# First attention stage of a hybrid decoder layer: pool layout, chained second minimum, inverse sums on GpSimd

## The chip, the cores and the metric

The kernel runs on one core of one Trainium2 chip. The metric is device microseconds of one execution, as the median of several runs; lower is better. The core has five instruction streams that run side by side, each in its own fixed order: TensorE (PE in the profile, with its weight loads as PEld), VectorE (DVE), ScalarE (ACT), GpSimd (POOL) and SyncE (SP, which only issues transfers). An instruction starts when the one before it on its engine has gone and the semaphores that it names have come.

## The reference, cut to what matters

One decoder layer over 1024 tokens of width 1024. A token mixer with two head groups is followed by a SwiGLU network. The change lies in group A (8 heads, 2 key groups of 4 heads), whose output is a gated sum of three softmax attentions:

```python
p_c = _masked_softmax(einsum(qg, kc) * scale, mask_c)      # 63 compressed keys per head
imp = einsum(p_c, overlap)                                 # picks 8 blocks of 64 keys per query
p_s = _masked_softmax(einsum(q_b, kg) * scale, mask_s)     # the selected blocks
p_w = _masked_softmax(einsum(q_b, kwb) * scale, mask_w)    # a sliding window of 512 keys
o = gt[:, :, 0] * o_cmp + gt[:, :, 1] * o_s + gt[:, :, 2] * o_w

def _masked_softmax(s, mask):
    s = where(mask, s, NEG_INF)
    e = where(mask, exp(s - max(s)), 0.0)
    return e / maximum(sum(e), 1e-30)
```

Group B (8 heads) is a second attention over 256 picked keys per query, with the same softmax.

## The kernel before, in words

The program is one long function. It runs in stages: conditioning and norm; projections with the top-k search of group B beside them; the first attention stage (group A); the second attention stage (group B, `DsaUnit`); output projection; the feed-forward network. A scheduler orders each engine's instructions from the written program by priorities, so the order of the source is not the order on an engine.

**The first attention stage** has 32 units, `NsaUnit(i, g, br)`: query tile `i` of 128 tokens (0 to 7), key group `g`, branch `br` (2 is the window, 1 the selected blocks). A unit has two halves. `head` (L804) makes four rows of scores, one per head. For each, `softmax_head` (L715) lets PE write scores of up to 512 keys into a PSUM tile `pS` (L721, L723), and DVE reads it once: one pass adds the mask, scales by -0.125, writes `p4` and leaves the row's minimum in `stat` (L729; the pass shows in the trace as a custom instruction and a short reading of its accumulator). With over 512 keys there are two passes, and a DVE instruction on one number per row takes the lesser of both minima (L731). Then ACT takes the exponential with the sum beside it (L732). `inv_sum` (L735) bounds the four sums from below (L736: on DVE for tiles 0 to 3, on POOL from tile 4 on) and inverts them on DVE (L737), and POOL scales the four rows by inverse and gate (L825). `tail` (L829) turns 128 keys at a time on PE (L837), splits them into two halves for accuracy on ACT (L741) and DVE (L742), and multiplies them with the values `VV` (L841, L842). `cmp_tile(i)` (L749) does the compressed branch of a tile for all 8 heads at once, with its own sums of 128x8 (L766 to L771). Heads run two units ahead of tails.

While tiles 0 to 3 run, DVE also writes the last masks of the top-k search (`masks`, L490 to L508).

**Memory.** Pools are stacks on two sides of the on-chip memory. At the end of the projections the right-hand pools `wk` (scratch of the rotation: `rt1`, `rt2`, `tke`), `wstream` (weights `wsp`, raw weights `raw`) and `hT` (the normed input, read by every projection) are closed, and `OT0`, `nsaK` and `att` are opened over their places. An instruction that writes a tile of a new pool waits for the last use of whatever old tile lay there. In the kernel before, tiles of `att` get their places in the order in which the code first asks for them: the first queries `qst` come to lie over `rt1`, `rt2` and `tke`, and the masks `wmask`, `maskc`, `identr`, `trir` over `hT`. At the far end of the stage the pools of the second attention stage lie over those of the first: the raw output weights `rawo1` over `oev`, which POOL reads last of all (L857).

## Time and profile before

| what | value |
|---|---|
| median of 3 runs | 1550.92 us (1549.51 to 1552.92) |
| the profiled execution, its own time | 1550.34 us |
| span of its profile | 1548.4 us |
| PE busy | 93% of the span |
| DVE busy | 76% |
| ACT busy | 57% |
| POOL busy | 45% |
| the chain that ended last | PE 59%, DVE 22%, DMA 6%, ACT 6%, issue 5%, POOL 3% |

Shares over the whole span mix stages with different limits. The first attention stage runs from about 352 to 636 us, the second from there to about 810 us. Times in the trace count from the start of the span.

### The profile page before, as it was taken

Reading aid. Unit: us, or ns where it says so; the run is one execution under the profiler, and the core shown is the slowest. Engines: PE = TensorE matmul, PEld = TensorE weight load, DVE = VectorE, ACT = ScalarE, POOL = GpSimd, SP = SyncE. Lnnn points to the kernel's source line nnn. Section 1 sums busy time; section 2 is a strip of 40 time slices with the busy share of each in tenths; the row PEclk is TensorE's granted clock in tenths of the full one; section 3 lists DMA queues with packets and bytes.
Section 4 is the critical chain, followed back from the end, with each engine's and each line's share of the span. In section 5 each row is a group of like instructions: output and inputs, shape, how many; then the busy total and the mean of one; then the engine's idle time right before and its main releaser. Section 6 shows DMA issues by size and latency. Waiting matters only on the chain.

```text
span 1548.4 us, 23692 instructions
## 1 busy us (share of the span) xinstructions
PE 1439.0 (93%) x7841; PEld 1222.6 (79%) x7841; DVE 1183.7 (76%) x2650; ACT 877.8 (57%) x1848; POOL 703.9 (45%) x978
## 2 busy tenths in 40 slices
PE   3799998996789999899998997999999999999998
PEld 3789898996667877788886785888878888788886
DVE  6888988997999999777865667675775555597757
ACT  3547669876877887677864874222332323354543
POOL 2584353546877666455544524663544353000003
PEclk9999999997999999999999898999999999999999
DMA  9471261200000000210125564542453331784336
GB/s 306 145 246 28 42 175 34 84 11 9 9 12 2 1 13 33 85 35 21 55 69 200 175 222 150 176 147 94 154 165 101 97 109 61 253 276 119 100 111 231
DMA packets 143002, 168.66 MB, mean 109 GB/s; under 512 B 17616, under 2 KB 92720, under 8 KB 142752
## 3 DMA queue, kind: packets, MB, share of 16 engines
q1 hardware_dynamic: 132256, 147.79, 30.3%
q10 hardware_dynamic: 9984, 17.24, 3.3%
q0 software_dynamic: 640, 2.13, 0.5%
q8 instruction: 61, 1.00, 0.3%
q14 instruction: 61, 0.50, 0.1%
HBM read 126.71 MB, written 40.41 MB: 108 GB/s over the span
## 4 chain that ended last, share of the span: by engine, by line
PE 59%; DVE 22%; DMA 6%; ACT 6%; issue 5%; POOL 3%; ACTq 0%; DVEq 0%; SPq 0%; POOLq 0%
PE pT L1158 11%; PE pO L1158 8%; PE pS L1158 6%; PE pT L1400 4%; PE pO L1400 4%; PE pS L1400 3%; DVE tk_j L470 3%; DVE p L729 3%; DVE ptl L742 2%; PE pT L837 2%; PE pO L272 2%; PE pS L721 2%; PE pO L274 2%; PE pO L273 2%; DMA wt<-in_w_ada_dram 2%
## 5 line engine op out<-in xcount | busy, mean ns | idle before, releaser
L742 DVE TENSOR_TENSOR ptl<-pT,ptl 128x512 fp32r<-128x512 f32 x228 | 139.7, 626 | 31.6 <-ACT ptl L741 30.6
L741 ACT CAST ptl<-pT 128x512 fp32r<-128x512 f32 x228 | 117.7, 541 | 40.8 <-PE pO L842 17.7
L1158 PE MATMUL pO<-hbs,wgu 128*128 128x512 f32 x564 | 137.8, 390 | 0.0
L118 ACT CAST wgu<-pair 128x512 fp32r<-128x512 f32 x88 | 53.7, 620 | 137.2 <-PE pT L1158 75.3
L272 PE MATMUL pO<-wsp,hT 128*128 128x256 f32 (+1 forms) x416 | 120.7, 292 | 9.7 <-ACT kvt L607 4.3
L1158 PE MATMUL pT<-hbs,wgu 128*128 128x512 f32 x528 | 127.1, 389 | 1.7 <-DVE u L1305 1.2
L273 PE MATMUL pO<-wsp,hT 128*128 128x256 f32 (+1 forms) x416 | 119.9, 289 | 5.1 <-DVE wsp L121 5.1
L1158 PEld LDWEIGHTS pO<-hbs,wgu 128*128 128x128 f32 x564 | 106.0, 188 | 22.1
L274 PE MATMUL pO<-wsp,hT 128*128 128x256 f32 (+1 forms) x416 | 119.1, 287 | 0.0
L1158 PEld LDWEIGHTS pT<-hbs,wgu 128*128 128x128 f32 x528 | 98.9, 188 | 23.1 <-DVE u L1305 1.6
L825 POOL TENSOR_SCALAR p<-p,stat,gates 128x640 f32<-128x640 f32 (+7 forms) x128 | 106.2, 844 | 23.2 <-DVE stat L737 17.8
L732 ACT ACTIVATE p<-p,stat 128x640 f32<-128x640 f32 (+7 forms) x128 | 94.0, 736 | 26.7 <-DVE stat L731 17.4
L118 ACT CAST wgu<-rawg 128x512 fp32r<-128x512 f32 x66 | 40.9, 622 | 93.8 <-PE pT L1158 48.2
L538 ACT ACTIVATE tk_j<-scores,tk_s 128x384 bf16<-128x384 f32 (+2 forms) x93 | 87.1, 937 | 9.6 <-DVE tk_s L480 3.4
L272 PEld LDWEIGHTS pO<-wsp,hT 128*128 128x128 f32 x416 | 81.0, 196 | 11.8 <-ACT kvt L607 4.9
L118 ACT CAST hl<-adr 128x512 fp32r<-128x512 f32 x77 | 47.4, 621 | 69.8 <-PE pO L1400 31.4
L273 PEld LDWEIGHTS pO<-wsp,hT 128*128 128x128 f32 x416 | 81.3, 196 | 6.7 <-DVE wsp L121 5.8
L121 DVE TENSOR_TENSOR wgu<-pair,wgu 128x512 fp32r<-128x512 f32 x88 | 71.5, 816 | 18.8 <-ACT wgu L118 18.2
L470 DVE TENSOR_SCALAR_CACHE_REDUCE tk_j<-scores,tk_v 128x512 bf16<-128x512 f32 (+2 forms) x96 | 83.9, 874 | 1.1 <-DMA mkd<-tk_j 0.5
L721 PE MATMUL pS<-KK,qst 128*128 128x512 f32 (+3 forms) x192 | 76.1, 402 | 8.3 <-DVE stat L729 8.0
L1411 POOL TENSOR_SCALAR ssd<-ssd 128x1 f32<-128x1 f32 x8 | 2.5, 310 | 178.4 <-ACT pT L1404 177.4
L837 PE MATMUL pT<-ident,p 128*128 128x128 f32 x528 | 81.7, 277 | 1.8 <-POOL p L825 1.2
(497 smaller groups left out, 4566.6 us busy)
## 6 DMA issues: line engine op xcount, KB each, us to landing
rawg<-in_w_gate_up_dram SPq DMA_DIRECT2D x102, 256.0 KB, 3.3
adr<-asd SPq DMA_DIRECT2D x77, 256.0 KB, 2.7
asd<-act SPq DMA_DIRECT2D x66, 256.0 KB, 2.5
raw<-in_w_in_dram SPq DMA_DIRECT2D x36, 256.0 KB, 2.9
xt<-in_x_dram SPq DMA_DIRECT2D x16, 512.0 KB, 6.1
wt<-in_w_ada_dram SPq DMA_DIRECT2D x32, 256.0 KB, 4.4
wt<-in_w_ada_dram SPq DMA_DIRECT2D x16, 512.0 KB, 5.2
we<-in_w_down_dram SPq DMA_DIRECT2D x22, 256.0 KB, 4.8
```

Of the source, the lines that this page charges most:

```text
L118: S.copy(hi, src)
L272: PE.matmul(o, lh, rh, start=first, stop=False)
L273: PE.matmul(o, lh, rl, start=False, stop=False)
L274: PE.matmul(o, ll, rh, start=False, stop=last)
L470: V.tensor_scalar(tkj[0][:, :w], score(i0 + j), thr(j), 0.0, op0=op, op1=OP.add, accum_out=cnt[:, j:j + 1])
L721: PE.matmul(s[:, :c1 - c0], q, kh[:, c0:c1], start=True, stop=False)
L741: S.copy(hl[:n_rows, 0, :width], src[:n_rows, :width])
L742: V.tensor_tensor(hl[:n_rows, 1, :width], src[:n_rows, :width], hl[:n_rows, 0, :width].bitcast(F32), op=OP.subtract)
L825: G.tensor_scalar(self.p4[:, r, :n], self.p4[:, r, :n], stat[:, 2, r:r + 1], gates[:, i, c0 + r:c0 + r + 1], op0=OP.mult, op1=OP.mult)
L837: PE.transpose(pt[:, r * P:(r + 1) * P], self.p4[:, r, k * P:(k + 1) * P], ident)
L1158: PE.matmul(bank, blk[:, a, k, :], hb[:, k, b, :], start=first and k + a + b == 0, stop=k == KH_ - 1 and a == 1, skip_group_check=True)
L1400: PE.matmul(bank[j], A[:, a, j * P:(j + 1) * P], B[:, b, :], start=first and k + a + b == 0, stop=last and k == NP - 1 and a == 1, skip_gr ...
```

## The change

It has three parts.

1. **Places.** `VV` is opened first and all other tiles of the stage go into `att` in the reverse of the order of the table `ATT`, before anything is written. In the built program the first `qst` now lie over the scratch of an earlier projection and the first weight tile of `wstream`, `wmask` over weight tiles, `ce`, `qhl`, `identr` and `trir` over `raw`, and the two large `p4_1` over `hT`; at the other end `rawo0`, `rawo1` and `ohl` of the second stage lie over the second `p4_1`, and no longer over `oev`.
2. **Second minimum.** The second pass over a row starts its minimum from the first pass's result, and writes the row's minimum itself; L731 goes. `softmax_head` also serves the second attention stage.
3. **Inverse sums.** In the first stage POOL takes the bound of all tiles and raises the sums to the power -1 (`OP.pow` with a constant tile), in the units (128x4) and in `cmp_tile` (128x8), where it also multiplies the gate. The second stage keeps its reciprocal on DVE.

```diff
@@ -97,8 +97,10 @@
     addc = cs[:, 320:384].rearrange("p (t e) -> p t e", t=4)
     V.memset(ones, 1.0)
     G.affine_select(ident, ones, pattern=[[1, P]], compare_op=OP.is_equal, fill=0.0, base=0, channel_multiplier=-1)
-    half = cp.tile([P, 4], F32, name="half")
-    V.memset(half, -0.5)
+    half = cp.tile([P, 8], F32, name="half")
+    V.memset(half[:, 0:4], -0.5)
+    V.memset(half[:, 4:8], -1.0)
+    inv = half[:, 4:8]
     tri2 = cp.tile([P, 256], BF, name="tri2")
     tri = tri2[:, 128:]
     G.memset(tri2, 0.0)
@@ -692,11 +694,23 @@
     otp = [R.push("OT0")]
     OT = [otp[0].tile([P, 4, SEQ], F32, name="OT0", tag="o")]
     rK = R.push("nsaK")
-    wmask = rK.tile([P, 640], BF, name="wmask")
-    maskc = rK.tile([P, NT, 64], BF, name="maskc")
-    mask01 = rK.tile([P, 1, 64], BF, name="mask01")
-    trir = rK.tile([P, P], F32R, name="trir")
-    identr = rK.tile([P, P], F32R, name="identr")
+    VV = rK.tile([P, NT, 4, P], F32R, name="VV")
+    at = R.push("att")
+
+    ATT = {"p4_1": ([P, 4, 1024], F32, 2), "trir": ([P, P], F32R, 1), "identr": ([P, P], F32R, 1),
+           "qhl": ([P, 4, 2, 64], F32R, 1), "ce": ([P, 8, 64], F32, 2), "wmask": ([P, 640], BF, 1),
+           "p4_2": ([P, 4, 640], F32, 2), "maskc": ([P, NT, 64], BF, 1), "mask01": ([P, 1, 64], BF, 1),
+           "qst": ([P, 4, P], F32R, 4), "stat": ([P, 4, 4], F32, 4), "st8": ([P, 4, 8], F32, 2),
+           "mr": ([P, 2, 16], F32, 2), "m8": ([P, 2, 8], F32, 2), "imb": ([P, 2, 16], F32, 2),
+           "imh": ([P, 2, 64], F32, 2), "ceh": ([P, 4, 2, 64], F32R, 2), "oev": ([64, 2, 512], F32, 1)}
+
+    def att(name):
+        shape, dt, n = ATT[name]
+        return at.tile(shape, dt, name=name, bufs=n)
+
+    for name in reversed(ATT):
+        att(name)
+    wmask, maskc, mask01, trir, identr = (att(n) for n in ("wmask", "maskc", "mask01", "trir", "identr"))
     G.tensor_copy(identr, ident)
     G.tensor_copy(trir, tri)
     G.memset(maskc, 0.0)
@@ -709,8 +723,6 @@
     G.tensor_copy(wmask[:, 512:], tri)
     G.affine_select(wmask[:, :128], wmask[:, :128], pattern=[[1, P]], compare_op=OP.is_gt, fill=NEG, base=0,
                     channel_multiplier=-1)
-    VV = rK.tile([P, NT, 4, P], F32R, name="VV")
-    at = R.push("att")
     psum_pool("psumB", 512, *ATT_PS)
 
     def softmax_head(p_, q, kh, kl, n, mask, stat, r, diag=False):
@@ -726,15 +738,18 @@
             out_, in_, mk_ = p_[:, c0:c1], s[:, :c1 - c0], mask(c0, c1)
             if diag:
                 out_, in_ = (a.rearrange("p (b e) -> p b e", e=64) for a in (out_, in_))
-            last = V.tensor_tensor_reduce(out_, in_, mk_, -0.125, 3e38, OP.add, OP.min, stat[:, 3 * j, r:r + 1])
-        if n > 512:
-            V.tensor_tensor(stat[:, 0, r:r + 1], stat[:, 0, r:r + 1], stat[:, 3, r:r + 1], op=OP.min)
-        S.activation(p_, p_, AF.Exp, bias=stat[:, 0, r:r + 1], scale=-1.0, accum_out=stat[:, 1, r:r + 1])
+            least = stat[:, 3 * j, r:r + 1]
+            last = V.tensor_tensor_reduce(out_, in_, mk_, -0.125, stat[:, 0, r:r + 1] if j else 3e38, OP.add, OP.min,
+                                          least)
+        S.activation(p_, p_, AF.Exp, bias=least, scale=-1.0, accum_out=stat[:, 1, r:r + 1])
         return last
 
     def inv_sum(stat, eng):
-        eng.tensor_scalar(stat[:, 1, :], stat[:, 1, :], 1e-30, None, op0=OP.max)
-        V.reciprocal(stat[:, 2, :], stat[:, 1, :])
+        G.tensor_scalar(stat[:, 1, :], stat[:, 1, :], 1e-30, None, op0=OP.max)
+        if eng is V:
+            V.reciprocal(stat[:, 2, :], stat[:, 1, :])
+        else:
+            G.tensor_tensor(stat[:, 2, :], stat[:, 1, :], inv, op=OP.pow)
 
     def pT_split(pool, src, n_rows=P, width=512, nb=3):
         hl = pool.tile([P, 2, 512], F32R, name="ptl", bufs=nb)
@@ -765,9 +780,9 @@
             G.tensor_tensor(e, e, mask01.to_broadcast([P, 8, 64]), op=OP.mult)
         V.tensor_reduce(st8[:, 1, :], e, AX.X, OP.add)
         G.tensor_scalar(st8[:, 1, :], st8[:, 1, :], 1e-30, None, op0=OP.max)
-        V.reciprocal(st8[:, 2, :], st8[:, 1, :])
+        G.tensor_tensor(st8[:, 2, :], st8[:, 1, :], inv[:, 0:1].to_broadcast([P, 8]), op=OP.pow)
         if i < 4:
-            V.tensor_tensor(st8[:, 2, :], st8[:, 2, :], gates[:, i, 0:8], op=OP.mult)
+            G.tensor_tensor(st8[:, 2, :], st8[:, 2, :], gates[:, i, 0:8], op=OP.mult)
         G.tensor_tensor(e, e, st8[:, 2, :, None].to_broadcast([P, 8, 64]), op=OP.mult)
         masks = None
         if i >= 4:
@@ -819,7 +834,7 @@
             if self.br == 1:
                 self.eh = at.tile([P, 4, 2, 64], F32R, name="ceh", bufs=2)
                 split(self.eh[:, :, 0, :], self.eh[:, :, 1, :], CM[i][1][:, 4 * g:4 * g + 4, :], S, G)
-            inv_sum(stat, V if i < 4 else G)
+            inv_sum(stat, G)
             c0 = self.br * 8 + 4 * g
             for r in range(4):
                 G.tensor_scalar(self.p4[:, r, :n], self.p4[:, r, :n], stat[:, 2, r:r + 1],
@@ -1024,7 +1039,7 @@
                 mk_ = tri2[:, 128 - P * i:] if i < 2 else score(i, mk)
                 mask = lambda a, b: mk_[:, a:b]
                 softmax_head(self.p4[:, j, :n], qs[tg][:, j, :], KH[:, 0, :], KH[:, 1, :], n, mask, stat, j)
-            inv_sum(stat, G)
+            inv_sum(stat, V)
             for j in range(4):
                 n = (4 * tg + j + 1) * P
                 G.tensor_scalar(self.p4[:, j, :n], self.p4[:, j, :n], stat[:, 2, j:j + 1], 1.0, op0=OP.mult, op1=OP.mult)
```

On POOL, at the start of the stage, the order before (`nqt` is the query tile, L294 to L297 its rotation; `tke` and `mkd` belong to the top-k masks):

```order
L702 MEMSET maskc 128x512
L705 MEMSET mask_4639 128x64
L708 MEMSET wmask 128x512
L709 COPY wmask<-tri_77 128x128
L294 TENSOR_TENSOR rt_4621<-nqt,cs 128x64
L295 TENSOR_TENSOR rt_4622<-nqt,cs 128x4x8
L296 TENSOR_TENSOR rt_4622<-nqt,cs 128x4x8
L703 AFFINE_SELECT maskc<-maskc 128x512
L706 AFFINE_SELECT mask_4639<-mask_4639 128x64
L710 AFFINE_SELECT wmask<-wmask 128x128
L297 TENSOR_TENSOR nqt<-rt_4621,rt_4622 128x4x16
```

and of the change:

```order
L510 DMA mkd<-tke 128x896
L296 TENSOR_TENSOR rt_4622<-nqt,cs 128x64
L297 TENSOR_TENSOR rt_4623<-nqt,cs 128x4x8
L298 TENSOR_TENSOR rt_4623<-nqt,cs 128x4x8
L299 TENSOR_TENSOR nqt<-rt_4622,rt_4623 128x4x16
L714 CAST identr<-ident 128x128
L715 CAST trir<-tri_78 128x128
L716 MEMSET maskc 128x512
L719 MEMSET mask_4662 128x64
L722 MEMSET wmask 128x512
L723 COPY wmask<-tri_78 128x128
L717 AFFINE_SELECT maskc<-maskc 128x512
```

The last rotation now stands ahead of the making of the masks, whose last step is the selection on `wmask` (L724, two rows on); the work is the same.

On ACT at the same place, with the semaphores that each waits for, before:

```order
L305 COPY nqt<-pS 128x256 [waits PE_49]
L402 CAST qst<-pT 64x2x128 [waits PE_49,DMASW0_49,Activation_49,Pool_49]
L403 CAST qst<-pT 64x2x128
L402 CAST qst<-pT 64x2x128 [waits PE_49]
L403 CAST qst<-pT 64x2x128
L118 CAST VV<-kvt 128x8x2x64 x2
```

and of the change:

```order
L307 COPY nqt<-pS 128x256 [waits PE_49]
L404 CAST qst<-pT 64x2x128 [waits DMAHW3_49,DMAHW7_49,PE_49,Pool_49]
L405 CAST qst<-pT 64x2x128
L404 CAST qst<-pT 64x2x128 [waits PE_49]
L405 CAST qst<-pT 64x2x128
L120 CAST VV<-kvt 128x8x2x64 x2
```

The order stays; the first copy into `qst` waits for other transfers (DMAHW3 and DMAHW7 carried results and weights of the projections) and no longer for the one that reads `tke` (DMASW0).

On POOL in the units of tile 0 and 1, before:

```order
L761 TENSOR_TENSOR ce_4696<-ce_4696,st8_4697 128x512
L825 TENSOR_SCALAR p4_2_4719<-p4_2_4719,stat_4720,gates_99 128x128 x4
L765 TENSOR_TENSOR ce_4696<-ce_4696,mask01_4639 128x512
L825 TENSOR_SCALAR p4_1_4747<-p4_1_4747,stat_4748,gates_99 128x128 x4
L121 TENSOR_TENSOR qhl_4828<-nqt_4026,qhl_4828 128x4x64
L508 DMA mkd_92<-tk_j0_487 128x384
L767 TENSOR_SCALAR st8_4697<-st8_4697 128x8
```

and of the change:

```order
L748 TENSOR_SCALAR stat_4739<-stat_4739 128x4
L752 TENSOR_TENSOR stat_4739<-stat_4739,half_75 128x4
L840 TENSOR_SCALAR p4_2_4738<-p4_2_4738,stat_4739,gates_100 128x128 x4
L776 TENSOR_TENSOR ce_4715<-ce_4715,st8_4716 128x512
L748 TENSOR_SCALAR stat_4767<-stat_4767 128x4
L123 TENSOR_TENSOR qhl_4847<-nqt_4027,qhl_4847 128x4x64
L752 TENSOR_TENSOR stat_4767<-stat_4767,half_75 128x4
L780 TENSOR_TENSOR ce_4715<-ce_4715,mask01_4662 128x512
L510 DMA mkd_93<-tk_j0_488 128x384
L840 TENSOR_SCALAR p4_1_4766<-p4_1_4766,stat_4767,gates_100 128x128 x4
L748 TENSOR_SCALAR stat_4798<-stat_4798 128x4
L782 TENSOR_SCALAR st8_4716<-st8_4716 128x8
```

Each set of four scalings now has a bound (L748) and a power (L752) ahead of it in POOL's own queue.

## Rows read from the trace of the kernel before

**Rows 1.** The page: busy time, share of the span and instructions, all engines.

```profile
PE 1439.0 (93%) x7841; PEld 1222.6 (79%) x7841; DVE 1183.7 (76%) x2650; ACT 877.8 (57%) x1848; POOL 703.9 (45%) x978
```

**Rows 2.** Stretches: length, then busy time (count) of PE, PEld, DVE, ACT, POOL; clock; DMA.

```profile
363.20:465.00 101.80, 84.20 (x453) 66.46 (x452) 96.37 (x280) 79.12 (x214) 80.58 (x111) 0.89 0.03 9
465.00:625.00 160.00, 153.60 (x944) 125.34 (x943) 150.90 (x484) 124.40 (x253) 106.36 (x144) 1.00 0.05 16
...
652.00:810.00 158.00, 154.44 (x895) 129.89 (x894) 125.45 (x372) 119.90 (x276) 81.16 (x124) 1.00 0.14 46
```

**Rows 3.** Waits from 355 to 465 us: who for whom; total us, times, longest.

```profile
POOL p L825 <- DVE stat L737: 6.8, 4, 4.2
...
PE pS L721 <- DVE stat L729: 5.3, 8, 1.3
```

**Rows 4.** Waits from 465 to 625 us.

```profile
ACT p L732 <- DVE stat L731: 15.5, 18, 2.7
```

**Rows 5.** Timeline of POOL at the start: start, us, instruction, idle before and releaser.

```profile
355.44 0.30 POOL L700 CAST identr<-ident 128x128 fp32r<-128x128 f32 x1
...
358.70 0.28 POOL L710 TENSOR_SCALAR_AFFINE_SELECT wmask<-wmask 128x128 bf16<-128x128 bf16 x1
358.97 0.31 POOL L297 TENSOR_TENSOR nqt<-rt,rt 128x64 f32<-128x64 f32 x1
```

**Rows 6.** Timeline of PE, ACT and DVE at the same place.

```profile
354.72 0.41 PE L399 MATMUL pT<-ident,nqt 128*128 128x128 f32 x2 [1.63 <-ACT nqt L305]
360.62 0.64 PE L755 MATMUL pT<-KKc,qst 128*128 128x64 f32 x2 [5.49 <-DVE qst L404]
...
359.31 0.37 ACT L402 CAST qst<-pT 64x256 fp32r<-64x256 f32 x1 [4.74 <-POOL nqt L297]
...
363.21 0.29 DVE L729 CUSTOM_DVE_ANT_0 p<-pS,wmask 128x128 f32<-128x128 f32 x1
```

**Rows 7.** DVE's groups from 363 to 625 us: count, busy us, mean ns, idle before.

```profile
L731 DVE TENSOR_TENSOR stat<-stat 128x1 f32<-128x1 f32 x64 | 20.9, 331 | 0.2
...
L736 DVE TENSOR_SCALAR stat<-stat 128x4 f32<-128x4 f32 x16 | 7.0, 440 | 0.0
...
L737 DVE RECIPROCAL stat<-stat 128x4 f32<-128x4 f32 x32 | 5.3, 166 | 0.7 <-POOL stat L736 0.5
```

**Rows 8.** Timeline of DVE at a row with two passes.

```profile
462.09 0.16 DVE L731 TENSOR_TENSOR stat<-stat 128x1 f32<-128x1 f32 x1
462.17 0.28 DVE L729 CUSTOM_DVE_ANT_0 p<-pS,wmask 128x128 f32<-128x128 f32 x1
```

**Rows 9.** Line 127, powers on POOL: ns least, median and most, first and last start.

```profile
L127 POOL TENSOR_TENSOR rxr<-rxv,half x8: 549/722/1355, 10.1 to 46.9; 128x1 f32<-128x1 f32 x8
...
L127 POOL TENSOR_TENSOR rcr<-rcv,half x2: 1115/1561/2007, 74.0 to 87.6; 128x4 f32<-128x4 f32 x2
```

**Rows 10.** Line 736, the bound of the sums, the same columns.

```profile
L736 DVE TENSOR_SCALAR stat<-stat x16: 134/242/1561, 368.4 to 456.4; 128x4 f32<-128x4 f32 x16
L736 POOL TENSOR_SCALAR stat<-stat x16: 219/220/225, 465.8 to 618.9; 128x4 f32<-128x4 f32 x16
```

**Rows 11.** Timeline of POOL at the cheaper power.

```profile
73.97 1.11 POOL L127 TENSOR_TENSOR rcr<-rcv,half 128x4 f32<-128x4 f32 x1
74.98 0.46 POOL L297 TENSOR_TENSOR g<-rt,rt 128x128 f32<-128x128 f32 x1
```

**Rows 12.** POOL's groups from 363 to 465 us: the scaling in its 128x256 form.

```profile
L825 POOL TENSOR_SCALAR p<-p,stat,gates 128x256 f32<-128x256 f32 x16 | 11.6, 736 | 0.0
```

**Rows 13.** Line 825, the scaling, all forms: ns least, median and most.

```profile
L825 POOL TENSOR_SCALAR p<-p,stat,gates x128: 442/878/2425, 370.1 to 623.0; 128x640 f32<-128x640 f32 x40, 128x128 f32<-128x128 f32 x16, 128x256 f32<-128x256 f32 x16, 128x384 f32<-128x384 f32 x16
```

**Rows 14.** The chain that ended last, between the two attention stages.

```profile
639.79 2.56 DMA rawo<-in_w_out_dram
```

**Rows 15.** Timeline of PE at the same place.

```profile
644.24 1.01 PE L1000 MATMUL pT<-ident,dqp 128*128 128x128 f32 x4 [2.43 <-DVE krT L939]
```

## The prediction

> **What bounds the kernel now.** I read the page first: over the whole span DVE is busy 76% and POOL 45% [rows 1]. These are averages over unlike stages, so the second view is the table of stretches, cut where the work changes [rows 2]. It gives the first attention stage in two parts. Stretch A (363 to 465 us, tiles 0 to 3) has DVE busy 96.4 of 101.8 us, POOL 80.6 and PE 84.2: DVE sets the pace, and POOL is the next in line with only 21.2 us free. Stretch B (465 to 625 us, tiles 4 to 7) has PE at 153.6 of 160, DVE at 150.9 and POOL at 106.4: two engines are nearly full, POOL has room. The second stage (652 to 810 us) has PE at 154.4 of 158. The third view is the waits. In A, POOL stands 6.8 us for DVE's reciprocal (L737) and PE 5.3 us for DVE to read a score tile [rows 3]; in B, ACT stands 15.5 us for the lesser of two minima (L731) [rows 4]. The fourth is the timeline where the projections end and the stage starts: PE transposes the first queries at 354.7 us and multiplies them only at 360.6, since ACT may write them no sooner than 359.3, when POOL has ended the last rotation; the first reduction of scores runs at 363.2 [rows 5, 6].
>
> **The change, part by part.** The sum goes against the profiled execution, 1550.34 us, which is 0.6 us (0.04%) below the median, so no correction is made.
>
> *The start.* POOL makes the masks from 355.4 us and ends the last rotation at 358.97 + 0.31 = 359.3, without a pause [rows 5]. The same work in the new order ends at 359.3 too, now with `wmask`. The queries no longer lie over the rotation's scratch, so ACT can write them from about 355.1, when the transposes are through (354.72 + 0.41 [rows 6]), and copies, halves and scores run beside POOL. What the first reduction then waits for last is `wmask`, at 359.3 and not at 363.2: 3.9 us gained. The ends are 0 (another old tile holds the queries as long) and 3.9 (the mask cannot come sooner). I take 3.9, since all that stood in the gap is named by the rows. Late next is that mask.
>
> *Stretch A.* DVE loses 16 bounds, 7.0 us, and 16 of the 32 reciprocals, 5.3 / 2 = 2.7 us [rows 7]; four wide reciprocals and four gate products of one small size are under a microsecond more and left out. That is 9.7 us of DVE. No row has two passes in these tiles. POOL gains 16 bounds at 0.22 us [rows 10], 3.5 us; 16 powers of 128x4; four wide powers of 128x8; four gate products at a price like the bound's, 0.9 us. Powers stand in the trace at L127 alone: 128x1 takes 0.55 us at the least, 128x4 1.115 and 2.007 [rows 9]. These two are the ends. I take the cheaper, as the dearer lies in a place where DVE streams from memory at the same time, and by starts: the next instruction begins 74.98 - 73.97 = 1.01 us later [rows 11]. Sixteen make 16.2 us. For 128x8 I work out (1.115 - 0.549) / 3 = 0.19 us a column, 1.115 + 4 x 0.19 - 0.1 = 1.8 us, four of them 7.1. Together POOL gets 3.5 + 16.2 + 7.1 + 0.9 = 27.7 us and needs 80.6 + 27.7 = 108.3 us where the stretch has 101.8. DVE comes down to 86.7. So POOL takes DVE's place as the bound, and the stretch grows by 6.5 us. Behind a power on POOL stand the four scalings of its unit, then PE's transposes of the tail. Ends: -9.7 us (POOL fits, DVE's relief is all felt) and, with every power as the dearer row, 3.5 + 32.1 + 4 x 3.2 + 0.9 = 49.3 us on POOL, +28 us.
>
> *Stretch B.* DVE loses 64 lesser minima, 20.9 us, and 2.7 us of reciprocals [rows 7]. The chained pass adds a read of the first pass's result on the same engine. Nothing shows that operation. Its nearest row is L731, which waits for the same result: from its start to the next pass 0.08 us [rows 8], 0.33 us on average [rows 7]. These are the ends; I take 0.08, since the long ones are lengthened by something other than that result, and 64 x 0.08 = 5.1 us go back. DVE comes to 150.9 - 20.9 + 5.1 - 2.7 = 132.4 of 160 us. POOL comes to 106.4 + 16 x 1.01 + 4 x 1.8 = 129.8. PE keeps its 153.6 [rows 2], and with DVE out of its way I let the stretch shrink to that: 6.4 us gained. Ends: 0, and 18.5 us (DVE's whole relief, if PE's busy time holds as much hidden waiting).
>
> *The end of the stage.* The load of `rawo1` goes out at 639.8 us, right behind POOL's last sum of the heads [rows 14], because it lies over what that sum reads; ACT's queue holds the copy of that weight ahead of one that PE waits 2.4 us for [rows 15]. In the new places the load waits for neither. The load before it in the queue still has to land, so I take 0.5 us, between 0 and 2.4.
>
> *The second stage.* Another 32 lesser minima go. PE is busy 154.4 of 158 us, so at most 3.6 us can come of it; the cover is PE's filler work, the first half of the output projection. I take 1.5, with ends 0 and 3.6. Its reciprocals stay on DVE and cost what they did.
>
> *Sum.* -3.9 + 6.5 - 6.4 - 0.5 - 1.5 = -5.8 us, 1544.5 us.
>
> **The rivals.**
>
> *POOL becomes a wall (slower).* Mechanism: in tiles 0 to 3 POOL and DVE get in each other's way, so a power costs more than alone. For it: the same scaling of 128x256 takes 0.74 us on average [rows 12], and one scaling took 2.4 us where the least is 0.44 [rows 13]; a bound of four numbers on DVE takes from 0.13 to 1.56 us [rows 10]; one of the two powers is at 2.0. Against it: DVE's 16 bounds go, and they were part of this. Price: with the median of the two powers, 1.56 us, POOL gets 3.5 + 25.0 + 4 x 2.5 + 0.9 = 39.4 us in A and the stretch grows by 18.2; B starts late and gives 4; -3.9 + 18.2 - 4 - 0.5 - 1.5 = +8.3, 1558.6 us. It decides from where A costs 5.8 us more than I took: over 16 powers and four of 1.8 times the size, 0.25 us each, so from 1.26 us a power. The Trainium skill's page Perfetto Trace Analysis, section Optimizing Scalar/DVE Operations, says that GpSimd and DVE share a port to on-chip memory, so that moving work from one to the other might not help; by that rule this rival is the forecast, and the trace agrees in that both engines show the long rows just named.
>
> *POOL is not full (much faster).* Its 80.6 us hold waiting for DVE [rows 12, 13], and with DVE less busy this goes. Then A gains 9.7, B some 12, the second stage 2.5: -3.9 - 9.7 - 12 - 0.5 - 2.5 = -28.6, 1521.7 us. Against it: the work that lengthens POOL's rows, the masks of the top-k, stays.
>
> *The second minimum does not do what it says (no change).* If the chained pass waits for the first as long as L731 took, B and the second stage give nothing: -3.9 + 6.5 = +2.6, 1553 us. For it: in the order both passes of a row can be neighbours. Against it: at L731 the wait itself is 0.08 us.
>
> **How the numbers follow.** The forecast has 0.48, the wall 0.22, no change 0.17, much faster 0.13. About 0.2% (3.1 us) is what a measurement of this kernel can tell from no change. The forecast's own case runs from about 1538 to 1549, and a twelfth of it lies within 3.1 us of the old time. So faster is 0.44 + 0.13 = 0.57, the same 0.04 + 0.17 = 0.21, slower 0.22. The range from 1530 to 1558 leaves out most of the fastest case and the upper half of the wall.
>
> **What would show it.** Right: the first reduction near 359.5 us; in the stretch of tiles 0 to 3 POOL busier than DVE, powers near 1.1 us, and PE's transposes waiting for POOL's scaling; in tiles 4 to 7 ACT's wait for L731 gone and DVE at least 15 us less busy, with PE full. Wrong: powers of 1.3 us or more in the stage, a second pass that takes 0.3 us longer than a first of its size, the first queries still written at 359 us, or DVE still the fullest engine in tiles 0 to 3.

## The result and the profile after

The changed kernel takes 1559.83 us (median of 5 runs, 1558.28 to 1564.86) where the kernel before took 1549.51 beside it: ratio 1.0067 [1.0045, 1.0089]. The forecast was 1544.5 us.

| | before | after |
|---|---|---|
| span of the profile | 1548.4 us | 1558.1 us |
| first reduction of scores | 363.2 us | 357.3 us |
| from there to the end of tile 3's scaling (A) | 101.8 us | 115.5 us |
| from there to tile 7's last product (B) | 171.4 us | 173.1 us |
| last product of the stage to the second stage's first product of probabilities and values (L1044 before, L1059 after) | 28.0 us | 27.8 us |
| first to last such product of the second stage | 169.5 us | 170.4 us |

B ends here at the start of the last product, at 636.4 us before; the 465 to 625 us of [rows 2] lie inside it. The second stage's last product starts at 833.9 us before, behind the 810 of [rows 2].

The page of the changed kernel, busy time of all engines, to be held against [rows 1]:

```profile
PE 1440.7 (92%) x7841; PEld 1226.3 (79%) x7841; DVE 1163.5 (75%) x2495; ACT 879.9 (56%) x1848; POOL 756.9 (49%) x1038
```

Over the span DVE lost 20 us and POOL gained 53. The stretches tell more. A, B and two slices of A in the changed kernel (columns as in [rows 2]):

```profile
357.30:472.80 115.50, 85.54 (x434) 68.55 (x435) 87.32 (x233) 78.03 (x213) 110.52 (x154) 0.81 0.02 8
472.80:645.90 173.10, 166.44 (x1018) 137.05 (x1017) 150.98 (x420) 133.18 (x267) 131.43 (x167) 0.99 0.05 15
380.00:390.00 10.00, 2.88 (x10) 1.91 (x9) 8.10 (x20) 5.05 (x16) 9.52 (x15) 0.54 0.04 15
440.00:450.00 10.00, 4.38 (x15) 2.50 (x15) 3.48 (x10) 3.66 (x10) 10.00 (x14) 0.79 0.01 2
```

In A POOL is busy 110.5 of 115.5 us, DVE 87.3, PE 85.5. From 440 to 450 us POOL works without a break while every other engine is under half. POOL's own waits in A, all of them (who for whom; total us, times, longest):

```profile
POOL stat L748 <- ACT p L744: 0.6, 1, 0.6
```

Before, POOL stood 6.8 us for the reciprocals alone [rows 3]. Now it waits for hardly anybody: 110.5 us of work, 0.6 of waiting and 4.4 in gaps between its 154 instructions are the 115.5. None of these gaps is over 0.11 us. There are 56, and 31 of them stand beside one of the 16 bounds (L748) and make 2.6 us. Elsewhere, as between the four scalings of a unit, an instruction follows the one before it without a gap. In the kernel before there are 19 such gaps in A, 1.4 us. Who waits for it, in the waits from 357 to 475 us:

```profile
PEld pT L861 <- POOL ceh L123: 13.1, 3, 7.7
PE pT L861 <- POOL ceh L123: 12.0, 2, 7.4
ACT ce L777 <- POOL ce L776: 8.2, 3, 6.2
DVE ptl L864 <- PE pT L861: 6.6, 1, 6.6
```

`ceh` (L123) holds the halves of the compressed branch, which the first tails turn on PE (L861). POOL's timeline ahead of the first of them (start, us, instruction):

```profile
374.79 1.64 POOL L783 TENSOR_TENSOR st<-st,half 128x8 f32<-128x8 f32 x1
376.40 1.00 POOL L752 TENSOR_TENSOR stat<-stat,half 128x4 f32<-128x4 f32 x1
377.40 3.12 POOL L840 TENSOR_SCALAR p<-p,stat,gates 128x128 f32<-128x128 f32 x4
380.50 0.64 POOL L785 TENSOR_TENSOR st<-st,gates 128x8 f32<-128x8 f32 x1
...
384.76 1.13 POOL L786 TENSOR_TENSOR ce<-ce,st 128x512 f32<-128x512 f32 x1
...
387.62 1.04 POOL L752 TENSOR_TENSOR stat<-stat,half 128x4 f32<-128x4 f32 x1
388.74 0.64 POOL L782 TENSOR_SCALAR st<-st 128x8 f32<-128x8 f32 x1
389.46 2.85 POOL L123 TENSOR_TENSOR ceh<-ce,ceh 128x256 fp32r<-128x256 f32 x2
```

And PE's at the same place, where the bracket gives the idle time before and its releaser:

```profile
383.45 0.41 PE L735 MATMUL pS<-KK,qst 128*128 128x256 f32 x1
391.24 1.11 PE L861 MATMUL pT<-ident,ceh 128*128 128x128 f32 x4 [7.37 <-POOL ceh L123]
```

The compressed branch's inverse is there at 376.4 us, its gate only behind a power and four scalings at 380.5, its product at 384.8, its halves behind another power at 389.5; and PE does nothing for 7.37 us. The first product with the compressed values (L865, the "first tail" of the expectations) runs at 395 us, where it ran at 388 before (L850), although the stage had started 5.9 us sooner.

Prices of the added instructions, columns as in [rows 9]: the power of a unit, the wide power, the bound. Three groups of the changed kernel:

```profile
L752 POOL TENSOR_TENSOR stat<-stat,half x32: 996/1036/1821, 361.2 to 629.6; 128x4 f32<-128x4 f32 x32
...
L783 POOL TENSOR_TENSOR st<-st,half x8: 1633/1664/1665, 374.8 to 590.4; 128x8 f32<-128x8 f32 x8
...
L748 POOL TENSOR_SCALAR stat<-stat x32: 208/228/547, 360.6 to 629.3; 128x4 f32<-128x4 f32 x32
```

So the power has the price that was taken (1.01 us), and the wide one is a little cheaper than the 1.8 worked out. Two of the sixteen powers in A are longer, 1.42 and 1.82 us.

### The profile page after: what moved, and what is told of

Read it like the earlier page. It is cut to its first block, busy times and chain, and to the rows that moved or that the text cites. A ratio compares the mean times of both kernels' runs of the same rounds, so it can differ in the third digit from the quotient of the medians.

```text
span 1558.1 us, 23702 instructions
## 1 busy us (share of the span) xinstructions
PE 1440.7 (92%) x7841; PEld 1226.3 (79%) x7841; DVE 1163.5 (75%) x2495; ACT 879.9 (56%) x1848; POOL 756.9 (49%) x1038
## 5 line engine op out<-in xcount | busy, mean ns | idle before, releaser
L840 POOL TENSOR_SCALAR p<-p,stat,gates 128x640 f32<-128x640 f32 (+7 forms) x128 | 103.7, 823 | 1.4
L123 DVE TENSOR_TENSOR wgu<-pair,wgu 128x512 fp32r<-128x512 f32 x88 | 72.4, 827 | 18.8 <-ACT wgu L120 18.1
```

What stands on the lines that cost most here:

```text
L123: elo.tensor_tensor(lo, src, hi.bitcast(F32), op=OP.subtract)
L840: G.tensor_scalar(self.p4[:, r, :n], self.p4[:, r, :n], stat[:, 2, r:r + 1], gates[:, i, c0 + r:c0 + r + 1], op0=OP.mult, op1=OP.mult)
```

## The experiments

All times are medians, and each ratio is to the kernel before in runs on the same chip (its medians there 1550.8 to 1551.6 us, and 1549.5 beside the change). "Change" is the whole change, "its order" the order in which the change's engines run.

| kernel | us | ratio | A | POOL busy in A | B |
|---|---|---|---|---|---|
| the change | 1559.8 | 1.0067 [1.0045, 1.0089] | 115.5 | 110.5 | 173.1 |
| places alone | 1549.0 | 0.9986 [0.9974, 0.9999] | 104.2 | 79.4 | 174.1 |
| chained minimum alone | 1546.1 | 0.9979 [0.9965, 0.9992] | 104.3 | 80.6 | 167.1 |
| powers alone | 1572.2 | 1.0148 [1.0124, 1.0171] | 116.8 | 107.5 | 175.5 |
| places and chain | 1543.0 | 0.9955 [0.9934, 0.9975] | 104.1 | 80.4 | 168.7 |
| + power in the units | 1552.5 | 1.0000 [0.9990, 1.0011] | 110.5 | 103.4 | 170.9 |
| + power in the compressed branch | 1549.3 | 0.9986 [0.9973, 0.9998] | 106.5 | 88.9 | 170.7 |
| change, multiplications | 1540.5 | 0.9926 [0.9912, 0.9941] | 97.5 | 90.8 | 169.1 |
| + power from tile 4 on | 1546.4 | 0.9969 [0.9954, 0.9984] | 103.5 | 80.1 | 168.6 |
| its order, all cheap | 1546.5 | 0.9970 [0.9957, 0.9984] | 102.7 | 92.6 | 171.1 |
| other order, all powers | 1572.9 | 1.0134 [1.0115, 1.0153] | 116.5 | 110.1 | 181.7 |
| + spare powers | 1554.8 | 1.0019 [1.0004, 1.0034] | 111.9 | 93.7 | 170.7 |
| places and chain, no bound | 1549.2 | 0.9990 [0.9979, 1.0001] | 103.7 | 82.3 | 173.6 |
| its order, early ones cheap | 1549.7 | 0.9994 [0.9978, 1.0011] | 102.8 | 92.3 | 176.6 |
| its order, early units cheap | 1550.8 | 0.9998 [0.9984, 1.0013] | 104.0 | 99.1 | 174.4 |
| its order, early wide cheap | 1554.9 | 1.0026 [1.0010, 1.0042] | 111.0 | 105.1 | 171.9 |

A and B are of the one profiled execution, "+" means on top of places and chain. That execution can lie some us off the median: 1550.8 us against 1554.9 with the early wide powers cheap, 1542.8 against 1546.4 with powers from tile 4 on.

### The three parts apart

Each of the first three runs is the kernel before with one numbered part of the diff: the table `ATT` (places), the starting value of the second pass (chain), or the powers with their constant tile (powers). The fourth has the first two.

```diff
-    def inv_sum(stat, eng):
-        G.tensor_scalar(stat[:, 1, :], stat[:, 1, :], 1e-30, None, op0=OP.max)
-        if eng is V:
-            V.reciprocal(stat[:, 2, :], stat[:, 1, :])
-        else:
-            G.tensor_tensor(stat[:, 2, :], stat[:, 1, :], inv, op=OP.pow)
+    def inv_sum(stat, eng):
+        eng.tensor_scalar(stat[:, 1, :], stat[:, 1, :], 1e-30, None, op0=OP.max)
+        V.reciprocal(stat[:, 2, :], stat[:, 1, :])
```

(The fourth against the change; the compressed branch's inverse and gate go back to DVE in the same way.)

> The kernel before with the new places alone (part 1 of the change). Theory, POOL is the wall: the places cost nothing and bring the earlier first reduction (357.3 us in the changed kernel, 363.2 before), so 4 to 6 us under the kernel before, about 1544 to 1546 us. Rival, the places are at fault: some tile of the stage now waits longer for an old one, and the loss is already here, at or above 1555 us.

> The kernel before with the chained second minimum alone (part 2). Theory as forecast: VectorE loses some 16 us in tiles 4 to 7 and that is felt, 6 to 8 us under the kernel before. Rival, those tiles are paced by TensorE with its waits for ScalarE's copies: within 2 us of the kernel before although VectorE is busy 15 us less there.

> The kernel before with the inverse sums on GpSimd alone (part 3). Theory, POOL is the wall: this part alone loses, 10 to 16 us over the kernel before, with GpSimd over 92% busy in tiles 0 to 3. Rival, the power is only a loss in the new places, or the scheduler's order did it: within 4 us of the kernel before.

> The changed kernel with the inverse sums back on VectorE (parts 1 and 2, without 3). Theory, POOL is the wall: everything lost comes back and the start stays, 4 to 12 us under the kernel before, 1538 to 1546 us. Rival, places or chain are at fault: still above the kernel before.

Measured: 1549.0, 1546.1, 1572.2 and 1543.0 us. The powers alone lose 1.5%, the other two together win 0.45%, and that pair beats both kernels. Only the pair came out where it was expected: the places gave 1.8 us and not 4 to 6, the chain 4.7 and not 6 to 8, and the powers lost 21 us and not 10 to 16. The places bring the first reduction to 357.6 us, but the last product of tile 2 with the compressed values starts at 448.8 us where it started at 450.4, so most of the start is given back. The chain shortens B: its stretches in the run with the chain alone are

```profile
364.40:468.70 104.30, 88.07 (x452) 70.89 (x452) 95.54 (x278) 79.32 (x214) 80.64 (x111) 0.84 0.03 9
468.70:635.80 167.10, 161.59 (x1011) 134.73 (x1010) 151.12 (x436) 131.13 (x266) 108.89 (x147) 1.00 0.05 15
```

The kernel before has over its own B

```profile
465.00:636.40 171.40, 164.91 (x1011) 134.24 (x1009) 159.53 (x496) 131.92 (x266) 108.72 (x147) 1.00 0.05 15
```

B is 4.3 us shorter, and with the places as well it is 168.7 where the places alone have 174.1. DVE is busy 8.4 us less. PE idles 5.5 us where it idled 6.5, and the other 3.3 us come out of PE's busy time.

### Which of the powers, with a new order each time

"+ power in the units" and "+ power in the compressed branch" put one half of part 3 on top of places and chain. "+ power from tile 4 on" keeps DVE's bound and reciprocal in tiles 0 to 3 and in the compressed branch; of its edit against places and chain, the call (`inv_sum` takes the power where its third argument is true):

```diff
-            inv_sum(stat, V if i < 4 else G)
+            inv_sum(stat, V if i < 4 else G, i >= 4)
```

> The whole change with the compressed branch's inverse and gate put back on VectorE, so GpSimd gets in tiles 0 to 3 only the 16 bounds and the 16 powers of 128x4. Theory 'demand': the loss follows the microseconds that GpSimd must work between the first reduction and the end of tile 3's scaling. Here that is 80.4 (as in the places-and-chain run) + 16 x (1.07 + 0.23) = 101 of some 104 us, so the stretch gives way by half to two thirds of what the whole change does: about 109 us, and a time near 1550 (1546 to 1555). Rival 'queue of the first tails': the loss comes from the compressed branch's own power, which stands in GpSimd's in-order queue ahead of the products for the first tails; without it the first tail is back near 385 us and the time is within 2 us of 1543.

> The whole change with the inverses of the units as before (bound and reciprocal on VectorE in tiles 0 to 3, bound on GpSimd and reciprocal on VectorE from tile 4 on); only the compressed branch's inverse (8 powers of 128x8) and gate are on GpSimd. Theory 'demand': GpSimd has 80.4 + 4 x (1.66 + 0.25) = 88 us of work in a stretch of 104, it is not full, and the time stays at 1543 to 1546. Rival 'queue of the first tails': the power sits ahead of the products that the first tails need; the first tail is 5 us or more later (390 or later instead of 385), and the time is 1549 or more.

> The whole change without any power in tiles 0 to 3 and in the compressed branch: bound and reciprocal on VectorE there, and the power of 128x4 on GpSimd in the 16 units of tiles 4 to 7 alone. Theory 'the loss is made in tiles 0 to 3': GpSimd has 109 + 16 x 1.07 = 127 us of work in tiles 4 to 7's 169, far from full, and the time is that of the places-and-chain run, 1541 to 1546. Rival 'a power costs where it stands too': each power lengthens the chain from a group's sums to its scaling by about 0.9 us against the reciprocal, and tiles 4 to 7 grow by 4 us or more over 168.8; the time is 1547 to 1555.

Measured: 1552.5, 1549.3 and 1546.4 us. The units' powers cost what 'demand' said. With them only in late tiles B stays at 168.6 us in the profiled execution, the fastest of the run; the median, 1546.4, lies between the 1541 to 1546 of the theory and the 1547 to 1555 of its rival and settles neither. The compressed branch alone goes against 'demand': POOL has 88.9 of 106.5 us to do, the first tail runs at 392 us (385 in places and chain), and the time is the rival's. But that difference is 6 us, the scheduler lays a new order for each of the three, and what that alone is worth isn't known yet.

### Price and order apart

The multiplication run replaces `OP.pow` by `OP.mult` at both places (L752, L783) and does not compute the inverse. The first of the two:

```diff
-            G.tensor_tensor(stat[:, 2, :], stat[:, 1, :], inv, op=OP.pow)
+            G.tensor_tensor(stat[:, 2, :], stat[:, 1, :], inv, op=OP.mult)
```

> The whole change with a multiplication in the place of each of the two powers: the same instructions in the same queues in the same order, the inverse is not computed. Theory 'price of the power': with 0.2 to 0.3 us instead of 1.07 and 1.66 GpSimd's work before the end of tile 3's scaling falls from 110 to about 93 us of 104 to 106; the time comes within 3 us of the places-and-chain run, 1542 to 1547. Rival 'order': it is that the sums are waited for by GpSimd's in-order queue instead of by VectorE's; then the price does not matter and the time stays above 1553.

It takes 1540.5 us, less than the 1542 to 1547 of 'price', a ratio of 0.9926 where the change has 1.0067. But what was written ahead of it was wrong in one thing, the order did not stay: the scheduler laid another one, and in the traces near a thousand of PE's 7,841 instructions stand elsewhere. The next two runs keep the orders. The scheduler works on the one operation; when every engine's order is set, the 40 instructions are exchanged for the same ones with the other (`names` holds the 40; the lines that count them are left out):

```diff
+    for f in nc.m.functions:
+        for b in f.blocks:
+            L = list(b.instructions)
+            for k, i in enumerate(L):
+                if i.name in names:
+                    L[k] = type(i)(op=OP.mult, name=i.name, engine=i.engine, debug=i.debug, ins=i.ins, outs=i.outs,
+                                   descendants=i.descendants, sync_info=i.sync_info)
+                    ...
+            b.instructions = L
```

> The multiplication run before this (1540.5 us) also let the scheduler lay every engine's order anew, so price and order changed together. Here each engine's order is word for word that of the whole change, and only the 40 inverses (32 of 128x4, 8 of 128x8) are multiplications when they run; the inverse is not computed. Theory 'price': the order is as good as the other, and the time comes within 4 us of 1540.5, that is 1538 to 1545, with the stretch from the first reduction to the end of tile 3's scaling near 98 us. Rival 'order': the scheduler laid out a worse order around a GpSimd that it believes busy; then the time stays at 1552 to 1560. Between them (1546 to 1551) both have a share.

> The other half of the pair: each engine's order is word for word that of the multiplication run, but the 40 inverses are powers when they run, so it computes what the whole change computes. Theory 'price': 16 x 0.8 + 4 x 1.4 = 18 us more on GpSimd in tiles 0 to 3 than in the multiplication run, most of it on the path: 1552 to 1560. Rival 'order': 1541 to 1546, as in the multiplication run.

The order of the change with cheap inverses takes 1546.5 us (0.9970), with powers 1559.8 (1.0067). The other order takes 1540.5 (0.9926) and 1572.9 (1.0134). In either order the price alone is worth more than the whole loss: 1.0% in the one, 2.1% in the other. 'Price' holds: the second run is even above its 1552 to 1560, and the first, at 1546.5, lies in the zone where both have a share. The change's order is the better one with powers and the worse one without, as if the scheduler had already given way to them. The inverse of a unit in the run of the change's order, cheap:

```profile
L752 POOL TENSOR_TENSOR stat<-stat,half x32: 192/203/998, 362.7 to 616.3; 128x4 f32<-128x4 f32 x32
```

Its stretches A and B:

```profile
358.80:461.50 102.70, 84.46 (x431) 66.69 (x431) 88.16 (x232) 76.06 (x208) 92.58 (x153) 0.83 0.03 9
461.50:632.60 171.10, 165.47 (x1030) 137.20 (x1029) 149.77 (x420) 134.62 (x272) 112.60 (x167) 1.00 0.05 15
```

A is 12.8 us shorter than in the change, with POOL's work 17.9 us less; B only 2.0 us shorter, with 18.8 less. So most of the price is paid in tiles 0 to 3, and the slack of B covers most of it there. PE's wait for the halves of the compressed branch, 12.0 us in the change, is, in the same order with cheap inverses,

```profile
PE pT L861 <- POOL ceh L123: 3.7, 2, 2.7
```

The other order with powers, A and B:

```profile
361.40:477.90 116.50, 86.09 (x420) 71.56 (x420) 87.19 (x230) 75.31 (x207) 110.08 (x150) 0.75 0.02 8
477.90:659.60 181.70, 170.26 (x1040) 139.64 (x1039) 151.03 (x422) 134.16 (x272) 134.09 (x171) 0.98 0.05 14
```

Against the multiplications in that order (97.5 and 169.1 us) A grows by 19.0 us for 19.3 us of POOL's work, and B by 12.6 us for 19.6: what slack B has depends on the order.

The last three keep the change's order and make some of the powers cheap: those of tiles 0 to 3 with five wide ones, the units' among them, the wide ones among them.

> Every engine's order is that of the whole change (1559.8 us). The 16 powers of the units of tiles 0 to 3 and the 5 wide ones of the compressed branch that run beside them are multiplications (their inverses are not computed); the 16 powers of the units of tiles 4 to 7 and three wide ones stay. Theory 'tiles 0 to 3': the loss is made where GpSimd was busy 110.5 of 115.5 us; with these cheap the time is within 3 us of the run with all 40 cheap (1546.5), 1545 to 1550. Rival 'everywhere': the late powers take their share of 13.3 us, some 6 us, and the time is 1551 to 1555.

> As the run before this one, with only the 16 powers of the units of tiles 0 to 3 made cheap. Theory 'a microsecond is a microsecond': GpSimd loses 16 x 0.8 = 13 us of work, the wide ones 5 x 1.4 = 7; the gain over the whole change splits two to one, and the time is 1549 to 1553. Rival 'the wide ones alone count' (they stand ahead of the halves that the first tails wait for): 1556 or more.

> As the two before, with only the 5 wide powers of the compressed branch in tiles 0 to 4 made cheap. Theory 'a microsecond is a microsecond': 7 us less work on GpSimd, a third of the gain, 1554 to 1557. Rival 'the wide ones alone count': 1546 to 1550.

Measured: 1549.7, 1550.8 and 1554.9 us, all inside 'tiles 0 to 3' and 'a microsecond is a microsecond'. 'The wide ones alone count' is out, and the 6 us of the compressed branch alone, in an order of its own, are no sign of it. The early ones carry 0.73 of the 0.97% that all 40 are worth (1.0067 less 0.9994, less 0.9970). The late ones carry the other 0.24%, near what these runs can tell; with them alone B is 176.6 us, 5.5 longer than with all cheap, so B does not cover them for nothing. The early units alone give 9.0 us and the wide ones 5.0, and both together 10.2, less than their sum. Stretch A with the early units cheap, and then with the early wide ones cheap:

```profile
358.80:462.80 104.00, 83.94 (x431) 66.81 (x431) 87.87 (x232) 76.83 (x210) 99.06 (x153) 0.84 0.03 9
```

```profile
357.00:468.00 111.00, 86.82 (x436) 69.09 (x437) 86.98 (x233) 77.88 (x212) 105.12 (x155) 0.80 0.02 8
```

In one order, then, POOL's work of 92.6, 99.1, 105.1 and 110.5 us gives an A of 102.7, 104.0, 111.0 and 115.5. From 99 on the length is the work and 5 to 6 us; below, something else holds some 103, which is why the two parts together give less than their sum. What holds it was not looked for.

### Occupied or in the chain of a unit

The spare powers write a column that nobody reads in tiles 0 to 3; bound and reciprocal stay on DVE.

```diff
         V.reciprocal(stat[:, 2, :], stat[:, 1, :])
+        if eng is V:
+            G.tensor_tensor(stat[:, 3, :], stat[:, 1, :], inv, op=OP.pow)
```

> Places and chain (1543.0 us), with bound and reciprocal on VectorE as before; in tiles 0 to 3 GpSimd takes beside them 16 powers of 128x4 whose results nobody reads. GpSimd's work there goes from 80.4 to about 98 us, as in the run with the units' powers, but no scaling waits for a power. Theory 'GpSimd's hours': what counts is that the engine is occupied, and the time is 1548 to 1554, as with the units' powers (1552.5). Rival 'the chain of one unit': what counts is that bound, power and scaling follow one another on one engine; with the power on nobody's path the time stays at 1542 to 1546.

It takes 1554.8 us, a little over the 1548 to 1554 of 'GpSimd's hours' and 11.8 above places and chain: a power costs as much here when nothing waits for its result. It is not POOL's hours alone, though, since A is 111.9 us with 93.7 of work. POOL's waits in that stretch hold one that the change hasn't:

```profile
POOL stat L751 <- DVE stat L748: 2.3, 4, 1.3
```

The spare power waits for a sum, and all that is queued behind it waits too. That is 2.3 of the 18.2 us in which POOL has no work in this A. DVE is busy 96.3 us where places and chain have 93.0, and the order is new as well, so which of these made A 7.8 us longer stays open.

### A version for use

> A version for use: places and chain, without the bound from below of the units' sums. A row's least scaled score is taken off before the exponential, so one term is exp(0) and the sum is at least 1: the bound of 1e-30 never acts. It takes 16 x 0.32 us off VectorE in tiles 0 to 3 and 16 x 0.22 us off GpSimd in tiles 4 to 7 and the bounds of the second stage. If VectorE's work in tiles 0 to 3 (93 of 104 us in the places-and-chain run) decides there, 1538 to 1541; if the order of waits does, 1541 to 1545 and no difference that these runs can tell.

The run leaves out the bound in `inv_sum`. It takes 1549.2 us, 6 us more than places and chain, though it only takes instructions away: no expectation said that. A is as long (103.7 and 104.1 us), B 4.9 longer. The orders differ throughout, so this is laid to the scheduler's order, but that wasn't tried by itself. It says how far a difference of one edit can be trusted here where the order is laid anew: some 6 us. By that measure the places, the chain, the compressed branch's powers and the late powers, each by a run of its own, are not shown to be worth what their runs differ by; the pairs in one order are. The best version seen is places and chain, 1543.0 us, ratio 0.9955 [0.9934, 0.9975].

## Why the prediction was wrong, step by step

**The start** was small and came in the right direction, 363.2 to 357.3 us, 5.9 gained where 3.9 were taken, but not for the reason given:

```profile
357.32 0.29 DVE L742 CUSTOM_DVE_ANT_0 p<-pS,wmask 128x128 f32<-128x128 f32 x1 [0.18 <-POOL wmask L723]
```

The first reduction needs of `wmask` only the copy of `tri` (L723), through at 357.3. The selection, which the prediction waited for, ends at 359.3 as forecast, but makes a part that tile 0 does not read. Nor is the start set by the places alone: with the same places it is 359.3 in places and chain and 362.7 in the multiplication run, which is the fastest all the same.

**Stretch A is the first of two steps that failed**, in the sentence "So POOL takes DVE's place as the bound, and the stretch grows by 6.5 us". POOL did take it, and the prices were right: 29.9 us of work came to it where 27.7 were counted, a power at 1.04 us. But the stretch grew by 13.7 us, from 101.8 to 115.5. The sum took POOL's 108.3 us of work for the length of the stretch. The work came to 110.5, and a queue that hardly waits still has 4.4 us of gaps, with 0.6 of waiting. That is 7.2 us, the whole difference. The gaps are a term that the prediction put at nothing: a bound was counted at 0.22 us, and the gaps beside the bounds are 0.16 us for each. What stands in front in POOL's queue then decides who waits: the first tails, PE up to 7.4 us at a time; for the scalings, which the prediction named, PE waits 2.2 us in all. Not all of the 13.7 us is the powers': places and chain without them have 104.1 in A, 2.3 more than the kernel before, since the earlier start isn't kept; their order is another one.

**Stretch B** is the second step that failed, and by a little more: -6.4 taken, +1.7 measured. It failed in the sentence "PE keeps its 153.6 [rows 2], and with DVE out of its way I let the stretch shrink to that: 6.4 us gained". PE idles 6.5 us over B before and 6.7 after: the stretch did not shrink to PE's busy time. Three things are in it. The relief of DVE was too large: it was reckoned at 18.5 us, 15.8 of them for the second minimum, and DVE's busy time over B falls by 8.4 with the chain alone and by 8.5 with the whole change. The prediction took L731 at its mean of 0.33 us [rows 7]; the kernel before has it at

```profile
L731 DVE TENSOR_TENSOR stat<-stat x64: 91/160/1010, 459.3 to 615.6; 128x1 f32<-128x1 f32 x64
```

The long ones are no time that DVE gains: rows of DVE overlap, as in [rows 8], where the next pass starts 0.08 us into L731. Of the 21.2 us of all 64 rows only 12.5 lie where no other row of DVE does. From that goes what the chained pass takes more, 0.06 us each (128x128 at 0.344 us against 0.284 for the first pass of a row):

```profile
L742 DVE CUSTOM_DVE_ANT_0 p<-pS,wmask,stat x32: 332/344/353, 468.1 to 620.4; 128x128 f32<-128x128 f32 x32
```

12.5 - 64 x 0.06 = 8.7 us; over A and B together DVE's busy time falls by 9.2 with the chain alone. The 0.08 that the prediction gave back was near enough; the 0.33 that it took away was not. And ACT's wait fell by a third but did not go: in tiles 4 to 7 of the changed kernel

```profile
ACT p L744 <- DVE stat L742: 10.5, 19, 1.8
```

where L731 had held it for 15.5 us [rows 4]. ACT now waits for the second pass itself. The third is the order and the powers: the chain by itself gave 4.3 us in B, the change's order with cheap inverses 0.3, and with all powers in that order B is 2.0 us longer.

**The end of the stage and the second stage**: -0.5 and -1.5 taken, -0.2 and +0.9 measured. PE was nearly full in the second stage, as [rows 2] said, and an instruction less on DVE did not shorten it. With -0.5 us between the second stage and the network the terms are -5.9 + 13.7 + 1.7 - 0.2 + 0.9 - 0.5 = +9.7 us, the difference of the spans. With A as taken it would be +2.5 us, with B as taken +1.6; it took both misses to come out this slow.

**The rivals.** 'POOL becomes a wall' came true to 1.2 us in its time (1558.6), and not by its mechanism, so that was luck. It decided "from 1.26 us a power", and the power took 1.04; the two long ones in A make 1.2 us together. Its rule, that moving work between GpSimd and DVE might not help because they share a read port (the Trainium skill, Perfetto Trace Analysis, section Optimizing Scalar/DVE Operations), agrees in the outcome. The port as the reason isn't what these runs show: in one order DVE is busy 87.3 us in A with powers and 88.2 with multiplications, in the other 87.2 and 87.6. Whether the accesses of the two engines hold each other up elsewhere was not tried. 'The second minimum does not do what it says' is out in its mechanism, since the chained pass is 0.06 us longer and not 0.33; its outcome, that B gives nothing, came all the same. 'POOL is not full' was right on the waits, since the 6.8 us of standing for reciprocals went [rows 3], and wrong in that work filled them at once. Of the signs named ahead, POOL busier than DVE and powers near 1.1 us came; PE waited more for the halves than for POOL's scaling, ACT's wait in tiles 4 to 7 stayed, and DVE was not 15 us less busy there.

## What to carry to other kernels

An engine that the change fills to over 95%, as POOL here, can be the new wall, and its stretch is then as long as its work plus what lies between its instructions: here 110.5 us of work made 115.5. Ask of a move not only whether the work fits, but what stands behind it in the queue: the halves that PE needed for the first tails were no part of the change, and PE's wait for them went from 3.7 to 12.0 us with the powers. Rows of one engine can overlap, as DVE's do here, so count for an instruction taken away only the time in which its engine does nothing else: 12.5 of 21.2 us for the 64 lesser minima. Where a scheduler lays the order anew, part price from order by exchanging the operation after the order is set.

## What was not expected of the hardware

- A power on POOL costs by the column: 0.55 us for 128x1 [rows 9], 1.04 for 128x4, 1.66 for 128x8, where a multiplication of 128x4 takes 0.20. DVE's reciprocal took 0.17 [rows 7].
- POOL's short instructions are not free one behind another: each of the 16 bounds in A (0.23 us) brought gaps of some 0.08 us on its sides, 2.6 us of the 4.4, while the four scalings of a unit follow one another without a gap.
- A pass on DVE that starts its minimum from a result in memory takes 0.06 us more than one that starts from a constant: 0.344 against 0.284 us at 128x128.
- TensorE's granted clock was 0.54 from 380 to 390 us, near the lower of its two levels (0.5, that is 1.2 of 2.4 GHz), where PE was busy 2.9 of 10 us, and 0.81 over A, against 0.89 [rows 2]. The run with cheap inverses in the same order has 0.83, is 12.8 us shorter, and has only 1.1 us less of PE's busy time, so the clock is not where that time went.
